# Taps between two gates, and the chunk matrices' transfers in five portions

## The chip, the cores and the metric

The kernel runs on one core of a Trainium2 chip. TensorE (PE) multiplies, VectorE (DVE), ScalarE (ACT) and GpSimd (POOL) do the rest, and SyncE (SP) issues nearly all transfers; each engine works off its own queue of instructions in program order and waits in it for what others must finish first. The metric is the time of one execution on the device in microseconds (us). The profile is taken from one execution; the median is over three others.

## The reference

One layer of a diffusion backbone over 512 latent tokens and 256 context tokens of 1024 channels: token mixing, then a mixture of 16 experts. Token mixing has two branches on the same normalised input h. One is a bidirectional diagonal state-space layer (S5: 32 groups of 16 channels, 64 complex states each), the other differential attention with 4 heads. Each branch is projected to 1024 channels and weighed by a sigmoid gate, then comes one output projection.

```python
u, q, k, v, ga, gb = split_in(h @ p['w_in'])
uc, qc, kc, vc, gac, gbc = split_in(hc @ p['w_in'])
ya, yac = s5_mixer(uc, u, p, need_ctx_out)
...
yb = diff_attention(q, concat([kc, k]), concat([vc, v]), lam, p['da_subln'], lam_init)
m = jax.nn.sigmoid(ga) * (ya @ p['w_proj_a']) + jax.nn.sigmoid(gb) * (yb @ p['w_proj_b'])
x = x + g_m * rms_norm(m @ p['w_out'], p['norm_post_mix'])
...
x = x + g_f * rms_norm(ec_moe(h2, ...), p['norm_post_ffn'])
```

The state-space layer is, in each direction, `h[l] = a * h[l-1] + B u[l]` and `y[l] = C h[l]`, both directions summed, plus a diagonal term in u.

## The kernel before

The kernel takes the 768 tokens in 96 chunks of 8. What a chunk's own inputs give to its own outputs is a product with a fixed matrix of 128 x 128 for each group (8 tokens x 16 channels on either side): the chunk matrix. It is put together from the taps, the responses C a^t B for t = 0 to 7 in either direction. What earlier and later chunks give goes through the states, which a scan over the chunks carries along.

The stages around the change, in program order: the input projection u and the factors of the taps; the chunks' states (products "st"); gates 0 to 7 (the first half of the sigmoid gates, "gate"), with the scan on VectorE and the taps between them; v for the attention ("v"); the readout ("y"), which needs the scan's end and the chunk matrices; and then the gated unit, the projections, q and k, attention, the output projection and the experts, whose weights (403 MB) stream through a ring of places.

*Numbers in two parts.* A product in float32 is made in three passes of a faster format (PASSES): each operand is split into a high part (ScalarE's copy) and a low part (VectorE's subtraction, source minus high part). For the gates, `prep_gate` (L703 to 713) does the first at once and puts the second on the list `due`, and `second_parts()` (L252) works the list off where it is called, in VectorE's queue. For v, `parts(raw, None)` (L261 to 270) does the same into a place taken from the list of free ones.

*The gates.* `gate(n)` (L722 to 740) makes 24 products of 128 x 512 in two halves and stops after each; the second half ends with the tanh (L732) and the preparation of gate n + 2. The raw weights come two gates at a time into one tile, `graw` (`load_gate`, L697): the load for gates 4 and 5 is put on `due` by gate 1, that for gates 6 and 7 by gate 3, each behind the subtraction that reads the tile last. Between the halves the loop at L888 to 917 lets VectorE go on with the scan (`steps`), from gate 2 on, and takes one piece of the taps.

*The taps.* `taps()` (L842 to 869) is a generator of eight pieces: four of the first direction (48 small products each), four of the second (16 each). After each four, ScalarE copies the result to KS (L865); in the first direction GpSimd adds the diagonal term (L868). Pieces are taken after the halves of gates 2 to 5.

*The chunk matrices.* `mt_load()` (L874 to 884) brings the taps to where the chunk matrices need them by transfers within the chip's memory, all on SP's queue: 8 from KS into the place of BZ (an operand of the taps that is no longer needed; L879), then for s = 0 to 7 two or four from BZ into the two tiles MT (L882, L884), 30 in all. They are issued after gate 5, behind two loads of v's raw weights (L915, `fetch`, L240). After that KS and BZ are given back.

*The places.* `E` is a list of free places of 128 x 2048 numbers. `take` takes the first (or, with `late=True`, the last), `give` puts places back at its end; who takes a place waits until everything that uses it from before is done. Before gate 7 `parts` takes two places for v's first two weight tiles: by the order of the list these are those of KS and BZ. v's raw tile has the place that `graw` gave back. The copies on ScalarE for both tiles stand in its queue ahead of gate 7's tanh. Two of the v accumulators are the two banks that the gates use in turn, and the first v product goes into the bank of gate 7.

Of the kernel before, what the change touches and what calls it, by code (L numbers as in the profile page):

```python
# [33 lines left out]
def layer(ctx: ExitStack, tc: tile.TileContext, A, out):  # L34
# [12 lines left out]
    ctx.enter_context(tc.manual_schedule())  # L47


    E = deque("U5 L0 L1 U7 U10 U3 U9 L2 U8 U0 U6 L3 U1 U11 L4 L5 L6 L7 U4 U2".split())  # L50
    for k in range(12):
        up.tile([128, 2048], F32, name="place", tag=f"U{k}")
    tag_of, held = {}, {}
# [1 line left out]
    def take(name, late=False):  # L55

        tag = E.pop() if late else E.popleft()
        t = (up if tag[0] == "U" else regs).tile([128, 2048], F32, name=name, tag=tag)
        tag_of[id(t)], held[id(t)] = tag, t
        return t  # L60

    def give(*ts):
        for t in ts:
            E.append(tag_of.pop(id(t)))
            held.pop(id(t))
# [23 lines left out]
    def bank(name="b"):  # L89
        turn_[0] += 1  # L90
        if three[0] and turn_[0] % 3 == 0:
            return cbank(name)
        if three[0] is None:
            return pb.tile([128, 512], F32, name=name, tag="b")
        pair_[0] += 1
        return pb.tile([128, 512], F32, name=name, tag="bd"[pair_[0] % 2])
# [143 lines left out]
    def fetch(dst, c0, p):  # L240

        DMA.dma_start(out=dst.rearrange("p (k f) -> p k f", k=2),
                      in_=w_in[256 * p:256 * p + 256, c0:c0 + 512].rearrange("(k p) f -> p k f", p=128))
# [9 lines left out]
    def second_parts():  # L253

        while due:
            due.popleft()()
# [4 lines left out]
    def parts(raw, eng, k=2):  # L261

        t = take("wp")
        hi_, lo_ = t[:, 0:1024].bitcast(F32R), t[:, 1024:2048].bitcast(F32R)
        S.activation(hi_, raw, AF.Copy)
        if eng is None:
            due.append(lambda: lo(V, lo_, raw, hi_))
        else:
            lo(eng, lo_, raw, hi_)
        return t, [v.rearrange("p (k f) -> p k f", k=k) for v in (hi_, lo_)]  # L270
# [28 lines left out]
    BC_ = take("BC")  # L299
# [162 lines left out]
    cn_ = take("cn")  # L462
# [144 lines left out]
    fm = matrices(tl)  # L607
# [86 lines left out]
    def gate_done():  # L694
        give(*GW["w"])
# [26 lines left out]
    def gate(n, eng, get):  # L722

        sg = sga_ if n < 8 else sgb_
        if n % 4 == 0:
            sg.append(take("sg"))
        w = GW["wv"][n % 2]
        pg = get("gate")
        passes(pg, w, hh, range(4), 7)
        yield  # L730
        passes(pg, w, hh, range(4, 8), 7)
        S.activation(sg[-1][:, 512 * (n % 4):512 * (n % 4) + 512], pg, AF.Tanh, scale=0.5)  # L732
        if n % 8 < 6:
            prep_gate(n + 2, eng)
        if n < 8:
            if n in (1, 3):
                due.append(lambda: load_gate(n + 3))
        elif n < 13:
            load_gate(n + 3, 1)
        yield  # L740
# [9 lines left out]
    for dr in range(2):  # L750
        for gq in range(8):
            psx = bank("st")
            pv = psx[:, 0:384].rearrange("p (g r c) -> p g r c", g=2, r=2)
            for gi in range(2):
                gp = 2 * gq + gi
                for ri in range(2):
                    for par in range(2):
                        g = 16 * (gp // 8) + 8 * par + gp % 8
# [11 lines left out]
    BZ_ = take("BZ")  # L770
# [52 lines left out]
    def steps(n):  # L823
        while n > 0:
            n -= next(fscan, 99)
# [9 lines left out]
    KS_ = take("KS")  # L835
# [6 lines left out]
    def taps():  # L842

        for dr in range(2):
            pkv = bank("K").rearrange("p (g t h) -> p g t h", g=4, t=8)
            for gi in range(4):
                def lh(q, d, ri):
                    return BZ[:, ri, 16 * d + 4 * q + gi].rearrange("p a h -> p (a h)")
                if dr == 0:

                    for d in range(2):
                        for ri in range(2):
                            for q in range(4):
                                PE.matmul(pkv[32 * q:32 * q + 32, gi, 0], lh(q, d, ri),
                                          BC[:, 1, 0, 16 * d + 4 * q + gi] if ri == 0 else CN[:, 16 * d + 4 * q + gi],
                                          start=gi == d == ri == 0, stop=d == 1 and ri == 1, skip_group_check=True)
                j1 = 1 - dr
                for ri in range(2):
                    for q in range(4):
                        PE.matmul(pkv[32 * q:32 * q + 32, gi, j1:j1 + 7].rearrange("p t h -> p (t h)"), lh(q, dr, ri),  # L860
                                  CP[dr, ri][:, 128 * (4 * q + gi) + 16 * dr:128 * (4 * q + gi) + 16 * dr + 112],
                                  start=dr == 1 and gi == ri == 0, stop=ri == 1, skip_group_check=True)
                if gi == 3:
                    t0 = slice(0, 8 - dr)
                    S.activation(KS[:, dr, :, t0], pkv[:, :, t0], AF.Copy)  # L865
                    if dr == 0:

                        GP.tensor_tensor(KS[:, 0, :, 0], KS[:, 0, :, 0], eye, op=OP.add)  # L868
                yield


    MT_ = []

    def mt_load():  # L874

        K2 = [BZ_[32 * dr:32 * dr + 32].rearrange("p (g t h) -> p g t h", g=16, t=8) for dr in range(2)]
        for dr in range(2):
            for q in range(4):
                DMA.dma_start(out=K2[dr][:, 4 * q:4 * q + 4, 0:8 - dr], in_=KS[32 * q:32 * q + 32, dr, :, 0:8 - dr])  # L879
        for s in range(8):  # L880
            for par in range(2):
                DMA.dma_start(out=MT[par][16 * s:16 * s + 16, :, s:8], in_=K2[0][16 * par:16 * par + 16, :, 0:8 - s])  # L882
                if s:
                    DMA.dma_start(out=MT[par][16 * s:16 * s + 16, :, 0:s], in_=K2[1][16 * par:16 * par + 16, :, 7 - s:7])  # L884

    ft = taps()
    wv = []
    for n in range(8):  # L888
        if n == 7:
            wv += [parts(vraw[p], None) for p in range(2)]  # L890
        for half, _ in enumerate(gate(n, None, cobank)):
            if n > 1:
                steps(1.8)
            if half == 0 and n > 1:
                second_parts()
            if n > 1:
                next(ft, None)
        if n < 2:
            second_parts()
            steps(2)  # L900
        if n == 7:
            for p in range(2):
                fetch(vraw[p], 1536, p + 2)
        if n == 5:
            for _ in ft:
                pass
            give(BC_, cn_)
            second_parts()
            give(graw)
            MT_ += [take("MT") for _ in range(2)]  # L910
            MT = [m.rearrange("p (g t h) -> p g t h", g=16, t=8) for m in MT_]
            vraw_ = take("vraw")
            vraw = [vraw_[:, 1024 * p:1024 * p + 1024] for p in range(2)]
            for p in range(2):
                fetch(vraw[p], 1536, p)  # L915
            mt_load()
            give(KS_, BZ_)
    gate_done()


# [251 lines left out]
    for p in range(4):  # L1172
        t, w = kw.pop(0)
# [303 lines left out]
    for n in range(8, 16):  # L1477
        m = n % 8
# [39 lines left out]
    hx_ = take("hfT")  # L1518
    E.extend((("SR", 0), ("U2", 0)))
    lg, aff = (keep.tile([128, 4, NE], F32, name=n) for n in ("lg", "aff"))  # L1520
# [144 lines left out]
    give(*wo, *mp_[0], *mp_[1])  # L1665
    E = deque(t for t in E if isinstance(t, tuple) or t[0] != "U")
    upper.close()
    pr = ctx.enter_context(tc.tile_pool(name="pairs", bufs=1))
    E.extend(("P", i) for i in (0, 1, 4, 2, 3, 5))
    E.extend((("SR", 1), ("gm", 0)))  # L1670

# [36 lines left out]
    def room():  # L1708

        ones_ = []  # L1710
        for tag in E:
            if is_pair(tag):
                E.remove(tag)
                t = wl[:, 0:4096] if tag[0] == "SR" else pr.tile([128, 4096], F32, name="we", tag="P%d" % tag[1])
                return t, [t[:, 0:2048], t[:, 2048:4096]], [tag]
            ones_.append(tag)
            if len(ones_) == 2:
                break
        for tag in ones_:
            E.remove(tag)  # L1720
        return None, [regs.tile([128, 2048], F32, name="wh", tag=x) if isinstance(x, str) else wl[:, 4096:6144] if x[0] == "SR" else
                      gm_ if x[0] == "gm" else yp_.rearrange("p b d -> p (b d)") for x in ones_], ones_
# [112 lines left out]
    for e in range(NE - 1):  # L1835
# [3 lines left out]
        if e % 2:  # L1839
            if not facc:  # L1840
                for x in strs(2):
                    t = regs.tile([128, 2048], F32, name="facc", tag=x)
# [26 lines left out]
    for j in range(3):  # L1869
        n = H[j].stop - H[j].start  # L1870
# [3 lines left out]
        for q in range(16 // nk):  # L1874
            if not halves:
                done_w(tags)
                _, halves, tags = room()
            wv = halves.pop(0).rearrange("p (k f) -> p k f", k=nk)
            m = 1 + (q == 1 and j == 2)
# [3 lines left out]
            for k in range(nk):  # L1883
                kt = nk * q + k
                g = kt % 2
# [71 lines left out]
```

## Time and profile before

| | |
|---|---|
| Median of 3 runs | 1576.85 us (1575.78 to 1576.99) |
| The profiled execution | 1569.68 us, its span 1567.9 us |
| TensorE busy | 1363.2 us (87%), mean granted clock 0.948 |
| VectorE, ScalarE, GpSimd busy | 523.9, 288.5, 115.1 us |
| Moved by DMA | 467.49 MB, mean 298 GB/s |
| The chain that ended last | PE 60%, DMA 22%, DVE 11%, ACT 3% of the span |

A timeline row has the start and duration in us, the engine, the line of the kernel, the operation, what it writes <- what it reads, the number of instructions merged, and in brackets the idle time before it and what ended it. PEld is TensorE's weight load, SPq SP's queue; a row of SPq is the issue of a transfer, not the transfer. PEclk is the granted clock of TensorE as a share of the full one, 2.4 GHz; the lower level is 0.5. The DMA share is the mean of 16 engines, over 1 where packets overlap.

### The profile page before, as it was taken

To read this page: it belongs to the slowest core of one execution; us is meant where nothing else is said; L and a number is where in the kernel's file an instruction comes from. 1 tells how busy PE (TensorE), PEld (TensorE's weight loads), DVE (VectorE), ACT (ScalarE), POOL (GpSimd) and SP (SyncE) were. 2 spreads that over 40 slices of the span, in tenths; PEclk is the share of its full clock that TensorE was granted. 3 is DMA by queue.
4 is the path that set the end of the run, shared out by engine and by line. 5 is a ranking of instruction groups with operands and counts; after the bars stand their busy time and mean duration, and the time that the engine had idled before them with its cause. 6 is when DMAs were issued, how large, how long until landed. Compare 5 with 4: busy or idle time off the path is not lost.

```text
span 1567.9 us, 17525 instructions
## 1 busy us (share of the span) xinstructions
PE 1363.2 (87%) x7230; PEld 733.3 (47%) x7230; DVE 523.9 (33%) x1214; ACT 288.5 (18%) x562; POOL 115.1 (7%) x87
## 2 busy tenths in 40 slices
PE   5989398998986894999999999989989979879985
PEld 3776277886665583434334343333334334324322
DVE  5789262376555647002012111111111111111103
ACT  3482004255433331100000000000000000000002
POOL 2000002332123300000000000000000000000003
PEclk9999699999997896999999999999999999999998
DMA  9111813233543248799999999999999999999994
GB/s 330 49 55 55 111 38 98 68 121 94 204 172 122 56 175 340 313 427 427 418 427 428 426 427 427 426 428 427 427 427 427 427 427 427 427 426 427 428 411 161
DMA packets 79680, 467.49 MB, mean 298 GB/s; under 512 B 14468, under 2 KB 38208, under 8 KB 49360
## 3 DMA queue, kind: packets, MB, share of 16 engines
q1 hardware_dynamic: 78288, 464.12, 74.2%
q10 hardware_dynamic: 768, 2.13, 0.4%
q8 instruction: 57, 0.93, 0.2%
q0 software_dynamic: 544, 0.12, 0.0%
q14 instruction: 23, 0.19, 0.0%
HBM read 461.66 MB, written 2.10 MB: 296 GB/s over the span
## 4 chain that ended last, share of the span: by engine, by line
PE 60%; DMA 22%; DVE 11%; ACT 3%; issue 2%; SPq 1%; POOL 0%; DVEq 0%; ACTq 0%
PE gu L1782 16%; DMA we<-in_w_exp_up_dram 11%; PE yd L1814 10%; DMA we<-in_w_exp_down_dram 7%; PE gat L1752 5%; PE gate L718 4%; PE sca L1826 4%; PE wo L1624 3%; PE u L584 2%; DMA wl<-in_w_exp_up_dram 2%; PE v L584 1%; PE k L1145 1%; PE proj L718 1%; PE o L1334 1%; PE ada L1237 1%
## 5 line engine op out<-in xcount | busy, mean ns | idle before, releaser
L1782 PE MATMUL gu<-we,gm 128*64 128x512 f32 x752 | 166.7, 595 | 16.5 <-DMA we<-in_w_exp_up_dram 10.1
L1782 PE MATMUL gu<-we,gf 128*64 128x512 f32 x752 | 167.9, 599 | 13.7 <-DMA we<-in_w_exp_up_dram 9.0
L1793 DVE TENSOR_TENSOR hid<-hid,gu 128x512 f32<-128x512 f32 x32 | 22.0, 687 | 462.9 <-PE gu L1782 462.9
L1814 PE MATMUL yd<-we,hid 128*64 128x512 f32 x688 | 152.3, 594 | 5.3 <-DMA we<-in_w_exp_down_dram 5.0
L1782 PEld LDWEIGHTS gu<-we,gm 128*64 128x64 f32 x752 | 52.9, 137 | 128.7 <-issue 104.9
L1782 PEld LDWEIGHTS gu<-we,gf 128*64 128x64 f32 x752 | 53.2, 138 | 125.6 <-issue 103.3
L718 PE MATMUL gate<-hh,wsp 128*128 128x512 f32 x384 | 98.9, 412 | 9.8 <-ACT sg L732 6.0
L1814 PEld LDWEIGHTS yd<-we,hid 128*64 128x64 f32 x688 | 49.0, 137 | 101.3 <-issue 97.1
L718 PEld LDWEIGHTS gate<-hh,wsp 128*128 128x128 f32 x384 | 73.8, 197 | 27.6 <-ACT sg L732 6.8
L1752 PE MATMUL gat<-mo,x 128*128 128x128 f32 x512 | 76.1, 313 | 10.2 <-DVE mo L1744 10.2
L1819 DVE COPY mo<-yd 64x512 f32<-64x512 f32 x15 | 10.4, 694 | 222.8 <-ACT mo L1818 222.8
L1867 POOL TENSOR_TENSOR fin<-facc,gf 128x256 f32<-128x256 f32 (+1 forms) x12 | 10.6, 913 | 997.8 <-DMA we<-in_w_exp_down_dram 993.6
L1752 PEld LDWEIGHTS gat<-mo,x 128*128 128x128 f32 x512 | 71.8, 221 | 18.1 <-issue 15.2
L1790 ACT ACTIVATE hid<-gu 128x512 f32<-128x512 f32 x32 | 19.1, 597 | 300.3 <-PE gu L1782 300.3
L1826 PE MATMUL sca<-mo,gm 128*128 128x512 f32 (+1 forms) x136 | 61.6, 591 | 4.8 <-ACT mo L1818 4.8
L1782 PE MATMUL gu<-wl,gm 128*64 128x512 f32 x208 | 53.3, 660 | 2.9 <-DMA wl<-in_w_exp_up_dram 2.9
L1798 ACT COPY hid<-ht 128x512 f32<-128x512 f32 x16 | 9.4, 585 | 249.4 <-PE ht L1797 249.4
L1624 PE MATMUL wo<-wo,mp 128*128 128x512 f32 x192 | 47.4, 404 | 2.3 <-DVE at L1484 2.3
L1818 ACT ACTIVATE mo<-yd 64x512 f32<-64x512 f32 x15 | 8.8, 589 | 214.3 <-PE yd L1814 214.3
L1831 DVE TENSOR_TENSOR facc<-facc,sca 128x512 f32<-128x512 f32 (+1 forms) x60 | 38.6, 650 | 17.7 <-PE sca L1826 17.7
L1814 PE MATMUL yd<-wl,hid 128*64 128x512 f32 x192 | 44.4, 596 | 0.0
L1826 PEld LDWEIGHTS sca<-mo,gm 128*128 128x128 f32 x136 | 21.5, 188 | 44.4 <-DVE facc L1831 23.6
(443 smaller groups left out, 1806.6 us busy)
## 6 DMA issues: line engine op xcount, KB each, us to landing
we<-in_w_exp_gate_dram SPq DMA_DIRECT2D x47, 2048.0 KB, 32.2
we<-in_w_exp_up_dram SPq DMA_DIRECT2D x47, 2048.0 KB, 28.9
we<-in_w_exp_down_dram SPq DMA_DIRECT2D x43, 2048.0 KB, 25.8
araw<-in_w_ada_dram SPq DMA_DIRECT2D x16, 1024.0 KB, 6.5
wl<-in_w_exp_gate_dram SPq DMA_DIRECT2D x8, 2048.0 KB, 28.9
wl<-in_w_exp_down_dram SPq DMA_DIRECT2D x8, 2048.0 KB, 31.0
wl<-in_w_exp_up_dram SPq DMA_DIRECT2D x8, 2048.0 KB, 26.4
wh<-in_w_exp_gate_dram SPq DMA_DIRECT2D x10, 1024.0 KB, 33.1
```

The lines of the kernel that those rows point to most:

```text
L584: PE.matmul(ps, tok(a, i, kt), w[b][:, kt % 2], start=kt == first and n == 0, stop=kt == last and n == 2)
L718: PE.matmul(ps, w[:, a, kt], x[b][kt], start=kt == 0 and n == 0, stop=kt == last and n == 2)
L1145: PE.matmul(acc[h], w[a][:, k, 128 * (h % 2):128 * (h % 2) + 128], hx[b][kt], start=kt == 0 and n == 0, stop=kt == 7 and n == 2, skip_grou ...
L1237: PE.matmul(ps[32 * j:32 * j + 32], csz[:, kt], araw[kt % 2][:, 512 * j:512 * j + 512], start=kt == 0, stop=kt == 7, skip_group_check=True)
L1624: PE.matmul(po[j], mparts(a, kt)[:, 128 * i:128 * i + 128], wo[kt][:, D * b + 512 * j:D * b + 512 * j + 512].bitcast(F32R), start=kt == 0 ...
L1752: PE.matmul(pg, x1[i][:, nb(d)], oh[:, i].rearrange("p e s -> p (e s)"), start=i == 0, stop=i == 3)
L1782: PE.matmul(pq[b][64 * j:64 * j + 64], xst[e // 2 % 2][:, kt, e % 2], wv[:, c:c + 512], start=kt == 0, stop=kt == 7, skip_group_check=True)
L1790: S.activation(hid[0][:, 1 - e % 2, b], pq[b], AF.Silu)
L1793: V.tensor_tensor(act, act, pgu[1][b], op=OP.mult)
L1814: PE.matmul(py[64 * j:64 * j + 64], hT_[:, b, i, 64 * jf:64 * jf + 64], wv[:, c:c + 512], start=(q == 0 and i == 0), stop=(q == 3 and i == ...
L1826: PE.matmul(po, gm[:, g0:g0 + 128], yp_[:, ep % 2, c], start=True, stop=True)
L1831: V.tensor_tensor(dst, dst, po, op=OP.add)
```

## The change

All eight pieces of the taps are made after gate 1, before gate 2. The tiles MT are taken there too, and `mt_load` becomes a generator that stops before s = 0, 2, 4 and 6: the 8 transfers into BZ are issued after gate 2, those for s = 0 and 1 after gate 3, s = 2 and 3 after gate 4, s = 4 and 5 after gate 5, and s = 6 and 7 after gate 6. v's first two raw loads are issued after gate 5, behind the fourth portion. KS and BZ are given back after gate 6, still ahead of the two places that v's weight tiles take before gate 7, which are again those of KS and BZ. `vraw` is taken from the list's end, the place that `graw` gave back just before. The list of places begins in another order, so that some tiles of the front part lie elsewhere, and with them the second tile of tanh values, MT, x1 and gf.

```diff
--- before.py
+++ after.py
@@ -47,7 +47,7 @@
     ctx.enter_context(tc.manual_schedule())
 
 
-    E = deque("U5 L0 L1 U7 U10 U3 U9 L2 U8 U0 U6 L3 U1 U11 L4 L5 L6 L7 U4 U2".split())
+    E = deque("U5 U11 L0 U7 U10 U3 U9 L1 U8 U0 U6 L2 U1 L3 L4 L5 L6 L7 U4 U2".split())
     for k in range(12):
         up.tile([128, 2048], F32, name="place", tag=f"U{k}")
     tag_of, held = {}, {}
@@ -878,12 +878,13 @@
             for q in range(4):
                 DMA.dma_start(out=K2[dr][:, 4 * q:4 * q + 4, 0:8 - dr], in_=KS[32 * q:32 * q + 32, dr, :, 0:8 - dr])
         for s in range(8):
+            if s % 2 == 0:
+                yield
             for par in range(2):
                 DMA.dma_start(out=MT[par][16 * s:16 * s + 16, :, s:8], in_=K2[0][16 * par:16 * par + 16, :, 0:8 - s])
                 if s:
                     DMA.dma_start(out=MT[par][16 * s:16 * s + 16, :, 0:s], in_=K2[1][16 * par:16 * par + 16, :, 7 - s:7])
 
-    ft = taps()
     wv = []
     for n in range(8):
         if n == 7:
@@ -893,28 +894,30 @@
                 steps(1.8)
             if half == 0 and n > 1:
                 second_parts()
-            if n > 1:
-                next(ft, None)
         if n < 2:
             second_parts()
             steps(2)
+        if n == 1:
+            for _ in taps():
+                pass
+            give(BC_, cn_)
+            MT_ += [take("MT") for _ in range(2)]
+            MT = [m.rearrange("p (g t h) -> p g t h", g=16, t=8) for m in MT_]
+            fm = mt_load()
+        if n > 1:
+            next(fm, None)
+        if n == 6:
+            give(KS_, BZ_)
         if n == 7:
             for p in range(2):
                 fetch(vraw[p], 1536, p + 2)
         if n == 5:
-            for _ in ft:
-                pass
-            give(BC_, cn_)
             second_parts()
             give(graw)
-            MT_ += [take("MT") for _ in range(2)]
-            MT = [m.rearrange("p (g t h) -> p g t h", g=16, t=8) for m in MT_]
-            vraw_ = take("vraw")
+            vraw_ = take("vraw", late=True)
             vraw = [vraw_[:, 1024 * p:1024 * p + 1024] for p in range(2)]
             for p in range(2):
                 fetch(vraw[p], 1536, p)
-            mt_load()
-            give(KS_, BZ_)
     gate_done()
```

## Rows read from the trace of the kernel before

**Rows 1.** Waits, all engines, 100 to 262 us: waiter, line <- releaser: sum, times, longest.

```profile
PE v L584 <- ACT sg L732: 26.5, 1, 26.5
ACT wp L265 <- DMA MT<-BZ: 23.8, 1, 23.8
```

**Rows 2.** Timeline, PE and ACT, 155 to 198 us: start, duration, engine, line, operation.

```profile
155.85 11.22 PE L718 MATMUL gate<-hh,wsp 128*128 128x512 f32 x48
156.88 0.53 ACT L865 ACTIVATE KS<-K 128x448 f32<-128x448 f32 x1
...
167.12 1.06 ACT L265 ACTIVATE wp<-vraw 128x1024 fp32r<-128x1024 f32 x1 [4.85 <-DMA BZ<-KS]
...
191.96 1.06 ACT L265 ACTIVATE wp<-vraw 128x1024 fp32r<-128x1024 f32 x1 [23.79 <-DMA MT<-BZ]
...
193.56 4.73 PE L584 MATMUL v<-wp,hc 128*128 128x512 f32 x12 [26.49 <-ACT sg L732]
```

**Rows 3.** Timeline of SP's queue, 146 to 188 us.

```profile
146.33 0.37 SPq L699 DMA_DIRECT2D graw<-in_w_in_dram  x1
158.27 0.88 SPq L242 DMA_DIRECT2D vraw<-in_w_in_dram  x2
159.26 5.99 SPq L879 DMA_DIRECT2D BZ<-KS  x8
165.82 1.87 SPq L882 DMA_DIRECT2D MT<-BZ  x3
...
170.36 0.70 SPq L882 DMA_DIRECT2D MT<-BZ  x1
...
181.31 0.62 SPq L882 DMA_DIRECT2D MT<-BZ  x1
...
186.44 1.38 SPq L884 DMA_DIRECT2D MT<-BZ  x1
```

**Rows 4.** Chain that ended last, 184 to 230 us: start, duration, what.

```profile
186.44 5.45 DMA MT<-BZ
```

**Rows 5.** DMA issues, 100 to 262 us: KB each, median us from issue to landing.

```profile
graw<-in_w_in_dram SPq DMA_DIRECT2D x3, 1024.0 KB, 5.3
vraw<-in_w_in_dram SPq DMA_DIRECT2D x4, 512.0 KB, 4.5
...
BZ<-KS SPq DMA_DIRECT2D x4, 64.0 KB, 5.1
```

**Rows 6.** Timeline, PE and DVE, 124 to 157 us, between and during the gates.

```profile
124.66 1.21 DVE L259 TENSOR_TENSOR wsp<-graw,wsp 128x1024 fp32r<-128x1024 f32 x1
...
125.93 3.98 PE L718 MATMUL gate<-hh,wsp 128*128 128x512 f32 x10 [3.32 <-DVE wsp L259]
...
128.30 1.21 DVE L259 TENSOR_TENSOR wsp<-graw,wsp 128x1024 fp32r<-128x1024 f32 x1
...
129.84 0.16 PEld L854 LDWEIGHTS K<-BC,BZ 128*32 128x32 f32 x8 [0.36 <-issue]
...
130.64 3.02 PE L718 MATMUL gate<-hh,wsp 128*128 128x512 f32 x12
...
152.80 1.22 DVE L259 TENSOR_TENSOR wsp<-graw,wsp 128x1024 fp32r<-128x1024 f32 x1 [1.96 <-ACT wsp L709]
...
155.16 1.19 DVE L786 TENSOR_TENSOR SR<-SR,mm 128x992 f32<-128x992 f32 x1
```

**Rows 7.** Stretches: busy us of PE, PEld, DVE, ACT, POOL; PEclk, DMA share, GB/s.

```profile
193.50:198.00 4.50, 4.44 (x12) 3.55 (x13) 4.19 (x21) 0.01 (x1) 0.00 (x0) 0.58 0.35 117
...
181.00:184.00 3.00, 0.00 (x0) 0.00 (x0) 0.00 (x0) 0.00 (x0) 0.00 (x0) 0.50 1.50 74
```

**Rows 8.** SP's waits, 330 to 700 us, and a stretch of the expert stage.

```profile
SPq L1732 <- PE wo L1624: 43.9, 1, 43.9
...
800.00:1000.00 200.00, 191.64 (x892) 76.12 (x890) 30.65 (x64) 12.54 (x23) 0.00 (x0) 0.99 1.01 427
```

## The prediction

> **What bounds the kernel now.** I read the waits of the stretch from the gates to the attention first, longest first. Two of them stand at one place: TensorE before its first v product and ScalarE before a copy of v's weights [rows 1]. The timeline shows how they hang together [rows 2]. Gates 6 and 7 (48 products) start at 155.85 and take 11.22 us, so TensorE is done at 167.07. On ScalarE's queue the tanh of gate 7 (L732) stands behind the two copies of v's first weight tiles (L265). The first copy runs at 167.12, the second at 191.96; the tanh comes after it, and only then is the accumulator free that v's first product takes, at 193.56. TensorE stands for 26.49 us. The second copy writes the place that BZ held, so it waits for the last transfer that reads BZ: issued at 186.44, landed 5.45 us later [rows 3, 4]. The 30 transfers of the chunk matrices, and the 8 before them, are issued from 159.26 on, because the last part of the taps is copied at 156.88 [rows 2, 3]. So what bounds this stretch is SP's queue: 38 small issues in a row, behind data that come late.
>
> **The change, part by part.** The sum is made on the profiled execution (1569.68 us, span 1567.9); the median of the runs, 1576.85, lies 7.17 above it, and I carry that difference over as it is.
>
> *The taps in one piece.* They are the same 256 products as before, now between gates 1 and 2. There TensorE stands for 3.32 us today, until the subtraction of gate 2's weights ends (124.66+1.21=125.87) [rows 6]; the last factor that the taps need is made by VectorE before that subtraction, so it is in time. A tap of the first direction takes 0.63 us (129.84 to 130.64, less 0.17 of standing) [rows 6], one of the second has a third of its products. Eight at 0.63 and a change-over on each side (0.35+0.17) are 5.5 us from 122.6, so gate 2 starts at 128 at the latest, some 2 us later than today; in return the eight interruptions of gates 2 to 5 go, each at least 0.52. That the burst of 256 keeps the pace of 48 is not shown; at twice the time gate 2 starts at 133.6. I take 5.5, since the instructions are the same. Neither is on the path: VectorE has no standstill that a tap would end, and its subtractions for gates 4 to 7 stay where they are. The one for gate 5 ends at 146.3, when the load for gates 6 and 7 is issued; the one for gate 6 ends at 152.80+1.22=154.02 [rows 3, 6]. From there two gates of 5.61 us end at 165.2 at the latest. ScalarE copies the taps before gate 2's tanh, where it waits for TensorE anyway.
>
> *The transfers in five portions.* SP serves them in program order. Portion 0 (8 issues, taps to BZ) stands behind the load for gates 4 and 5, which waits for gate 3's subtraction (128.30+1.21=129.51); by the 6.56 us from 159.26 to 165.82 it is out at 136.5. Portion 1 (s = 0, 1; 6 issues, 165.82 to 170.36) is out at 141. The load for gates 6 and 7 follows at 146.33, as today: gate 5's subtraction holds it, not the portion, with 5 us to spare [rows 3, 6]. From here on each step is on the path. From 146.70: portions 2 and 3 (16 issues, 170.36 to 181.31 today, 10.95 us) end at 157.65. v's two loads wait until gate 7's subtraction has read the gates' raw tile; on VectorE it follows the scan's step that ends at 155.16+1.19=156.35, so 157.6, nearly the same moment. The two loads take 0.99 us (158.27 to 159.26): 158.64. Portion 4 (8 issues, 5.13 us from the first, 181.31, to the last, 186.44) makes its last issue at 163.77; with 5.45 us of landing BZ is free at 169.22 [rows 3, 4, 6]. From landing to copy it is 0.07 us, from copy to v's first product 193.56-191.96=1.60: v starts at 170.9 instead of 193.56. **That is -22.7 us.** TensorE still stands 6 us before v, and v still starts at the lower level of 1.2 GHz (0.58 granted over its first 4.5 us today) [rows 7]: no gain and no loss from the clock.
>
> Bounds of this chain. From below: 0.61 us per issue and nothing between them, and a landing of 4.5, that of v's loads [rows 5]; v at 169.1, and 1.9 us more if its first 12 products (4.73 us [rows 2]) run at the later 0.234: -26.4. From above: each group of issues waits in the DMA engines for the load in front of it (5.3 for the gates', 4.5 for v's [rows 5]): 146.33+5.3+10.95+4.5+5.13+5.45=177.7, v at 179.3: -14.2. I take the measured pitch and landing: the 8 issues that follow v's two loads directly today landed in 5.1 [rows 5], so loads ahead in the queue have cost little.
>
> The last landing is the term that the Trainium skill prices otherwise. "DMA: Bandwidth & Descriptors", section "Anatomy of one DMA", has about 2.0 us plus bytes/436e9 for a transfer (measured for another way of issuing, so an estimate here): 2.3 us for these 112 KB, and -25.9 in all. The row says 5.45, and I go by the row; the page's result is rival 3. Its section "Queues, rings and completion order" says that each DMA engine takes descriptors in ring order, which speaks against small transfers behind big loads: rival 1.
>
> *The rest.* v's raw tile had the gates' place before too, so taking it from the other end of the list changes nothing by itself. The new order of the free places gives the second tanh tile the place of cn, and the matrices those of WT and BC, all read for the last time by the taps or before. After v everything is one chain: the scan on VectorE (its next piece stands behind the same weights), readout, attention, expert weights. SP's first full expert load waits 43.9 us for products of the output projection, and the stream then runs at 427 GB/s: bound by transfers, but started by TensorE [rows 8]. So the whole gain reaches the end: 1569.68-22.7=1547.0 in the profile, **1576.85-22.7=1554.2** as median.
>
> **The rivals.**
> *1. The portions queue behind the big loads in the DMA engines* (chance 0.13). For it: late in the transfers the engines' share is 1.50, more than one packet in each [rows 7]. Against it: the 5.1 us behind v's loads [rows 5]. Time: v between 173.9 (landing not counted again) and 179.3: 1557.2 to 1562.6, middle 1560.
> *2. TensorE becomes the bound* (0.08). It stands some us before gates 4 and 6; if the clock falls there and stays at 1.2 GHz over both last gates, 48 products of 0.398 end at 173.1, v follows at 173.7: -19.9, 1557.0. Against it: after the 3.32 us only ten products were slow (3.98 us), 1.6 us in all [rows 6], and gate 7 would still be hidden.
> *3. Shorter landings* (0.06): -25.9, 1551.0.
> *4. No gain* (0.03): the copy waits on its place for another reason than these transfers, or a later transfer takes the gain back: 1576.9. For the second a transfer between 200 and 600 us would have to start by itself; SP's longest wait there names TensorE [rows 8].
> *5. Slower* (0.04). x1, gf and three of the free places that the expert weights turn through lie elsewhere. If that slowed the stream of 403 MB (16 experts of three 1024x2048 matrices of 4 bytes) from 427 GB/s, the gain would be gone at 417 (943 us become 966); at 412 the time is 1588. Against it: 427 is held whichever place is filled [rows 8].
>
> **How the numbers follow.** The forecast has 0.66, from 1552 to 1557. The range that should hold 8 in 10 takes in rivals 2 and 3 and the nearer half of rival 1: 1549.5 to 1561. Faster by over 0.2% (3 us, about what this measurement can tell from no change) are the forecast and rivals 1 to 3: 0.93; within 0.2%: 0.03; slower: 0.04.
>
> **What would show it.** The taps as one block before gate 2, without 3.3 us of standing; SP's issues of the chunk matrices in groups from about 137 to 164; ScalarE's second copy of v's weights at about 169 and v's first product at about 171; then every stage 22 to 23 us earlier. It is wrong if that copy waits to 174 or later, if the load for gates 6 and 7 is issued clearly after 146.4, if gate 7 ends after 169, or if the shift at v is not there at the end.

## The result, and the profile after

| kernel | median us of the runs | beside it, before | ratio (95% interval) | profiled execution, its span |
|---|---|---|---|---|
| changed, first comparison | 1554.9 (1553.47 to 1559.93) | 1576.92 (1575.78 to 1577.93) | 0.9866 [0.9843, 0.9890] | 1559.93, 1558.2 |
| changed, second comparison | 1555.38 (1552.82 to 1557.58) | 1574.67 (1571.53 to 1579.01) | 0.9876 [0.9858, 0.9893] | span 1553.6 |
| changed, third comparison | 1555.48 (1551.58 to 1557.36) | 1575.70 (1565.89 to 1579.06) | 0.9881 [0.9855, 0.9908] | span 1553.1 |

The change makes the kernel 1.2 to 1.3% faster, 19.3 to 22.0 us. 1554.2 was forecast. The place of the gain is the one forecast; its size at that place is not, as the profile shows.

The waits of the changed kernel, 100 to 262 us, in the columns of [rows 1]; lines behind the loop of the gates are numbered 3 higher than before:

```profile
PE v L584 <- ACT sg L732: 10.4, 1, 10.4
ACT wp L265 <- DMA MT<-BZ: 6.9, 1, 6.9
```

Both waits of [rows 1] are still there, 16.1 and 16.9 us shorter. The same pair, the same order: ScalarE's second copy for v still waits for BZ's place, and TensorE waits for the tanh behind that copy. TensorE's timeline (start, duration, line, operation, in brackets the idle time before and what ended it) answers to [rows 2] and [rows 6]:

```profile
122.93 0.26 PE L854 MATMUL K<-BC,BZ 128*32 128x16 f32 x8
...
125.20 2.10 PE L860 MATMUL K<-CP,BZ 128*32 128x112 f32 x78
127.23 11.63 PE L718 MATMUL gate<-hh,wsp 128*128 128x512 f32 x50
141.82 13.96 PE L718 MATMUL gate<-hh,wsp 128*128 128x512 f32 x48 [2.96 <-DVE wsp L259]
156.20 10.72 PE L718 MATMUL gate<-hh,wsp 128*128 128x512 f32 x46 [0.42 <-DVE wsp L259]
177.29 5.16 PE L584 MATMUL v<-wp,hc 128*128 128x512 f32 x12 [10.37 <-ACT sg L732]
```

The taps begin at 122.93 and gate 2 at 127.23, without standing: 4.3 us for the burst (granted clock 1.00 from 123 to 128), and the standstill of 3.32 before gate 2 [rows 6] is gone. Gate 7 ends at 166.92. v starts at 177.29 instead of 193.56. ScalarE between them:

```profile
167.75 1.06 ACT L265 ACTIVATE wp<-vraw 128x1024 fp32r<-128x1024 f32 x1 [5.63 <-DMA vraw<-in_w_in_dram]
175.70 1.06 ACT L265 ACTIVATE wp<-vraw 128x1024 fp32r<-128x1024 f32 x1 [6.89 <-DMA MT<-BZ]
176.66 0.58 ACT L732 ACTIVATE sg<-gate 128x512 f32<-128x512 f32 x1
```

SP's queue in the changed kernel, beside [rows 3]: the load for gates 6 and 7 (L699), the chunk matrices (L884, L886), v's two loads (L242).

```profile
147.17 0.39 SPq L699 DMA_DIRECT2D graw<-in_w_in_dram  x1
147.60 0.59 SPq L884 DMA_DIRECT2D MT<-BZ  x1
...
151.91 0.61 SPq L884 DMA_DIRECT2D MT<-BZ  x1
153.76 0.58 SPq L886 DMA_DIRECT2D MT<-BZ  x1
...
160.64 1.54 SPq L242 DMA_DIRECT2D vraw<-in_w_in_dram  x2
162.50 0.59 SPq L884 DMA_DIRECT2D MT<-BZ  x1
163.38 2.16 SPq L886 DMA_DIRECT2D MT<-BZ  x1
...
168.75 0.61 SPq L884 DMA_DIRECT2D MT<-BZ  x1
171.33 0.58 SPq L886 DMA_DIRECT2D MT<-BZ  x1
```

The last issue was forecast for 163.77; it comes at 171.33, after two gaps (151.91 to 153.76, 168.75 to 171.33) that [rows 3] did not have. What filled them stands in SP's own waits, 146 to 176 us (sum, times, longest):

```profile
SPq L699 <- DVE wsp L259: 4.5, 1, 4.5
SPq L886 <- DMA vraw<-in_w_in_dram: 2.0, 1, 2.0
SPq L886 <- DMA graw<-in_w_in_dram: 1.2, 1, 1.2
SPq L884 <- DMA MT<-BZ: 1.2, 3, 0.6
SPq L242 <- DVE sp L813: 1.0, 1, 1.0
```

and in the chain that ended last (start, duration, what):

```profile
147.17 6.58 DMA graw<-in_w_in_dram
153.75 0.02 issue
...
161.70 9.61 DMA vraw<-in_w_in_dram
171.32 0.02 issue
171.33 4.29 DMA MT<-BZ
```

A transfer of the chunk matrices reads nothing of graw or vraw, and still its issue waits for their landing: 147.17+6.58=153.75 and 161.70+9.61=171.31. Counted in SP's timeline, the issue that waits is each time the eighth behind the load; the last section says what holds it.

The first products of the stages, from the traces of these kernels (us):

| kernel | v | readout, from the states (L968) | gated unit | k (first weights) | output projection | last expert's output, first product | span |
|---|---|---|---|---|---|---|---|
| before, first profile | 193.6 | 221.3 | 254.8 | 291.7 | 541.6 | 1528.1 | 1567.9 |
| before, again | 191.7 | 220.2 | 253.7 | 290.6 | 538.4 | 1524.8 | 1566.2 |
| taps alone | 192.8 | 220.9 | 254.4 | 292.9 | 545.0 | 1531.5 | 1573.0 |
| changed, first | 177.3 | 205.5 | 239.1 | 277.6 | 529.8 | 1516.5 | 1558.2 |
| changed, second | 174.3 | 202.7 | 236.2 | 274.6 | 526.9 | 1513.7 | 1553.6 |
| changed, third | 175.3 | 203.6 | 237.1 | 275.5 | 524.9 | 1511.5 | 1553.1 |
| changed, second copy late | 169.9 | 198.4 | 232.0 | 268.8 | 515.4 | 1502.0 | 1543.7 |

### The profile page after: what moved, and what is told of

It is laid out like the page before. It is cut to its first block, busy times and chain, and to the rows that moved or that the text cites. A ratio compares the mean times of both kernels' runs of the same rounds, so it can differ in the third digit from the quotient of the medians.

```text
span 1558.2 us, 17528 instructions
## 1 busy us (share of the span) xinstructions
PE 1367.1 (88%) x7230; PEld 739.3 (47%) x7230; DVE 525.7 (34%) x1214; ACT 288.8 (19%) x562; POOL 114.9 (7%) x87
## 4 chain that ended last, share of the span: by engine, by line
PE 57%; DMA 24%; DVE 13%; ACT 3%; issue 2%; SPq 1%; POOL 0%; DVEq 0%; ACTq 0%
PE gu L1785 15%; DMA we<-in_w_exp_up_dram 11%; PE yd L1817 10%; DMA we<-in_w_exp_down_dram 8%; PE gat L1755 5%; PE sca L1829 4%; PE wo L1627 3%; PE gate L718 3%; DMA wl<-in_w_exp_up_dram 2%; PE u L584 2%; PE v L584 2%; PE k L1148 1%; PE proj L718 1%; PE o L1337 1%; PE ada L1240 1%
## 5 line engine op out<-in xcount | busy, mean ns | idle before, releaser
L1822 DVE COPY mo<-yd 64x512 f32<-64x512 f32 x15 | 10.4, 694 | 221.2 <-ACT mo L1821 221.2
```

## The experiments

My theory after the first profile: the mechanism is the one forecast, the chain on SP's queue was priced too short, and what is left of the wait is still BZ's place. Against it stood two questions: whether the changed schedule loses time behind v (there the first two profiles differ by 6.5 us: v to the span's end 1374.3 before, 1380.9 after), and whether the taps, the spacing of the portions or the loads for v carry the effect.

**The two kernels again.** Both unchanged, with a new profile each and many timed runs.

> The kernel before once more, for a second profile. In the first comparison the median fell by 22.0 us, but the two profiled executions differ by only 9.8 (1569.68 and 1559.93), though v's first product moved by 16.3. Theory A: a single execution varies by some us outside the changed stretch, mostly where TensorE's granted clock falls; then this profile has the state products' start at 98 to 99 and v's first product at 193 to 195 as before, but stages behind it that are 3 to 7 us longer than in the first profile, or differ at other places. Theory B: the changed kernel loses 6 us in the stages behind v by itself; then this profile repeats the first one's stages behind v within 1 us.

> The changed kernel once more. Theory A: from the state products to v's first product 78 us again (within 1.5), v's gap of about 10 us behind the tanh of gate 7, and in the stages behind v other lengths than in the first profile of the change (+0.6 to the gated unit, +1.6 to k, +2.4 from the scores to the output projection, +1.7 at the end). Theory B: the same losses at the same places. Median 1553 to 1557 by both.

Measured: before 1573.14 against 1574.67 for itself (ratio 0.9988 [0.9975, 1.0001]); changed 1555.38 (0.9876). From v to the span's end it is again 1374.6 and 1379.3. That alone looked like a loss in the changed kernel. The next kernel says otherwise.

**The taps alone.** The taps stand between gates 1 and 2 as in the change; all portions are issued behind v's loads, as before.

```diff
-        if n > 1:
-            next(fm, None)
-        if n == 6:
-            give(KS_, BZ_)
...
             for p in range(2):
                 fetch(vraw[p], 1536, p)
+            for _ in fm:
+                pass
+            give(KS_, BZ_)
```

> The changed kernel with the taps in one piece before gate 2, but all 38 transfers issued after gate 5 behind v's loads, as before the change. Theory: the taps are off the path and the gain is the transfers' alone; SP's issues run from about 159 to 187, v's first product at 192 to 194, the time 1574 to 1578, no difference from before. Rival: the eight interruptions of the gates cost TensorE time that counts; then 4 to 6 us less than before, 1571 to 1573.

Measured: 1574.95, ratio 1.0000 [0.9988, 1.0012]. TensorE's row at v:

```profile
192.79 5.00 PE L584 MATMUL v<-wp,hc 128*128 128x512 f32 x12 [28.00 <-ACT sg L732]
```

The taps are worth nothing by themselves: the gates end earlier and TensorE stands 28.00 us instead of 26.49. And this kernel, with before's time, takes 1380.2 us from v to the end, as long as the changed one. So a loss of 6.5 us in the changed schedule is ruled out, to within the interval of some 2 us: before's two profiles caught short executions (1569.68 and 1568.03, where its medians are 1573 to 1577).

**All transfers at once behind gate 2.**

```diff
-        if n > 1:
-            next(fm, None)
+        if n == 2:
+            for _ in fm:
+                pass
```

> The changed kernel with all 38 transfers issued in one go after gate 2. Theory: SP's queue is in order, so the load for gates 6 and 7 comes behind them, at about 158 instead of 146 to 147; the subtraction of gate 6 ends at about 166, gate 7 at 176 to 179, and v starts at 177 to 181, 2 to 5 us later than in the changed kernel: 1556 to 1561. Rival: the spacing has no effect, since BZ is free early; then v starts at 168 to 170 and the time is 1547 to 1549.

Measured: 1565.58, ratio 0.9947 [0.9926, 0.9967]; worse than I expected. SP first, then ScalarE's copy of the gates' weights, then TensorE, each from its own timeline:

```profile
159.82 0.53 SPq L699 DMA_DIRECT2D graw<-in_w_in_dram  x1
```

```profile
167.34 1.06 ACT L709 ACTIVATE wsp<-graw 128x1024 fp32r<-128x1024 f32 x1 [19.55 <-DMA graw<-in_w_in_dram]
```

```profile
168.45 14.11 PE L718 MATMUL gate<-hh,wsp 128*128 128x512 f32 x48 [15.91 <-ACT wsp L709]
183.25 3.01 PE L584 MATMUL v<-wp,hc 128*128 128x512 f32 x12 [0.69 <-ACT sg L732]
```

Here the load for gates 6 and 7 stands behind all the small transfers and is issued at 159.82 instead of 147.17; TensorE waits 15.91 us before gate 6, and v starts at 183.25. The wait has moved from v to gate 6. The five portions are what keeps that load in its time: more than half of the gain hangs on the spacing.

**v's loads behind portion 4.** This takes v's loads out from in front of the last portion.

```diff
         if n == 6:
             give(KS_, BZ_)
+            for p in range(2):
+                fetch(vraw[p], 1536, p)
...
-            for p in range(2):
-                fetch(vraw[p], 1536, p)
```

> The changed kernel with both of v's first loads behind the last portion of the chunk matrices' transfers instead of in front of it. In both profiles of the change the last issue came at 169.2 and 171.3, not at the predicted 163.8, and it waited for a load of v that had been issued eight issues earlier. Theory: each issue waits until the transfer eight issues before it has landed, so a big load in front holds a small transfer eight places behind; then the last issue of the portions comes at 164 to 166 here, BZ is free at 169 to 171, but v's loads now land at 171 to 174 and v's first product is at 174 to 177, so the time stays within 1553 to 1558. Rival: the small transfers fill the DMA engines by themselves; then the last issue stays at 168 to 171 and v goes to 177 or later.

Measured: 1556.33, ratio 0.9893 [0.9871, 0.9916]. SP and ScalarE:

```profile
162.35 2.38 SPq L884 DMA_DIRECT2D MT<-BZ  x1
...
167.79 0.83 SPq L886 DMA_DIRECT2D MT<-BZ  x1
168.73 8.76 SPq L242 DMA_DIRECT2D vraw<-in_w_in_dram  x4
```

```profile
173.50 1.06 ACT L265 ACTIVATE wp<-vraw 128x1024 fp32r<-128x1024 f32 x1 [10.27 <-DMA vraw<-in_w_in_dram]
```

No issue of a portion waits for v's loads now. The last one comes at 167.79, 3.5 us earlier than in the changed kernel's first profile and 1.4 earlier than in its second, and still 4 us behind the forecast. So v's loads are one part of the excess and not all of it: one issue still waits 2.3 us for the gates' load, and an issue of over 2 us (162.35) is there without them too. The copy now waits for v's load itself, and nothing is gained in time. How the excess divides between the waits for a landing and the fill of the DMA engines (share 1.20, 1.39, 1.01 in 3 us each from 158 on in the changed kernel) is settled only so far.

**The second copy behind the tanh of gate 7.** If the rest of the wait is BZ's place, the tanh need only stand ahead of the copy that waits for it: then TensorE starts v on its first part and the second part comes in time.

```diff
         if n == 7:
-            wv += [parts(vraw[p], None) for p in range(2)]
+            wv += [parts(vraw[0], None)]
+            wt = take("wp")
...
         if n == 7:
-            for p in range(2):
-                fetch(vraw[p], 1536, p + 2)
+            fetch(vraw[0], 1536, 2)
+            w1 = [wt[:, 1024 * r:1024 * r + 1024].bitcast(F32R) for r in range(2)]
+            S.activation(w1[0], vraw[1], AF.Copy)
+            steps(5)
+            lo(V, w1[1], vraw[1], w1[0])
+            wv.append((wt, [x.rearrange("p (k f) -> p k f", k=2) for x in w1]))
+            fetch(vraw[1], 1536, 3)
...
-        steps(5)
+        if p:
+            steps(5)
```

> The changed kernel with the tanh of gate 7 ahead of the second copy of v's weights, and that copy's subtraction behind the scan steps of v's first part. Theory: what is left of the wait before v is the place of BZ alone, read by the last transfer, with TensorE done at 167. Then v's first product starts after the first copy, at 168 to 170 instead of 177.3, VectorE's wait of 6.7 us before the second subtraction goes, and the time is 6 to 8 us below the changed kernel, 1547 to 1549. Rival: the transfers of the chunk matrices themselves, or the scan on VectorE, set the readout's start; then v starts earlier but the readout does not, and the time stays at 1554 to 1556.

Measured: 1547.87, ratio 0.9828 [0.9807, 0.9850]; 7.5 us less than the changed kernel on the same chip. ScalarE and TensorE:

```profile
168.29 1.06 ACT L265 ACTIVATE wp<-vraw 128x1024 fp32r<-128x1024 f32 x1 [4.66 <-DMA vraw<-in_w_in_dram]
169.25 0.58 ACT L732 ACTIVATE sg<-gate 128x512 f32<-128x512 f32 x1
174.81 1.06 ACT L915 ACTIVATE wp<-vraw 128x1024 fp32r<-128x1024 f32 x1 [4.98 <-DMA MT<-BZ]
```

```profile
169.89 0.49 PE L584 MATMUL v<-wp,hc 128*128 128x512 f32 x1 [1.45 <-ACT sg L732]
...
180.69 2.83 PE L584 MATMUL v<-wp,hc 128*128 128x512 f32 x11 [1.48 <-DVE wp L259]
```

The copy still waits for BZ until 174.81, but TensorE works on v's first part meanwhile, and 1.48 us are left in front of the second. v starts at 169.9, close to where it was forecast, by another order.

**The same order on the kernel before,** to see whether it does this by itself; the edit is the one above.

> The kernel before with one edit only: the tanh of gate 7 ahead of the second copy of v's weights, and that copy's subtraction behind the scan steps of v's first part. Theory: the transfers still land at 190 to 192, so v's first part (36 products, 9 to 10 us) moves into the standstill, v's first product comes at 168 to 171, and v's second part waits for the copy until 193 to 195: 8 to 10 us less than before, 1564 to 1567. Rival: the order on ScalarE's queue was the whole loss; then the time is that of the changed kernel or less, 1547 to 1556.

Measured: 1564.30, ratio 0.9950 [0.9930, 0.9969]. TensorE:

```profile
168.46 0.50 PE L584 MATMUL v<-wp,hc 128*128 128x512 f32 x1 [1.36 <-ACT sg L732]
...
192.94 0.79 PE L584 MATMUL v<-wp,hc 128*128 128x512 f32 x1 [13.88 <-ACT wp L905]
```

v starts even earlier, and its second part waits for BZ 13.88 us. The order alone is worth 8.0 us and the earlier transfers alone 19.3 to 22.0; both together 26.8, and 28.2 on the third chip below.

**v's second load behind portion 4, with the late copy.** The last step that looked open: only the half of v's load that is needed first stays in front of the last portion.

```diff
         if n == 6:
             give(KS_, BZ_)
+            fetch(vraw[1], 1536, 1)
...
-            for p in range(2):
-                fetch(vraw[p], 1536, p)
+            fetch(vraw[0], 1536, 0)
```

> The changed kernel with the tanh of gate 7 ahead of the second copy, as in the run before, and v's second load behind the last portion, only the first in front of it. Theory: v's first copy waited for its load until 168.3 there, which shared the DMA engines with the second load and the portions; alone it lands at 164 to 166, so v starts right behind gate 7, at 167 to 168.5, 1.5 to 3 us earlier, 1544.5 to 1547. Rival: VectorE's scan sets the readout's start by now; then v starts earlier and the time stays within 1547 to 1549.

Measured: 1553.47, ratio 0.9879 [0.9857, 0.9902], with single runs from 1545.65 to 1554.33. ScalarE:

```profile
168.51 1.06 ACT L265 ACTIVATE wp<-vraw 128x1024 fp32r<-128x1024 f32 x1 [7.74 <-DMA MT<-BZ]
```

The first copy starts at 168.51 instead of 168.29: nothing gained. The row names a transfer of the chunk matrices as what ended its wait, but v's first load, issued at 159.21, landed 9.28 us later, at 168.49, just ahead of the copy, and the transfer that the row means, issued at 165.09, landed only at 170.32. So the copy waited for v's load as before, and that load, now without the second behind it, took longer than the 6.85 us of the run before, not less as I had expected. As the runs lay 9 us apart, three kernels were timed side by side on a third chip.

> The changed kernel, for a comparison on one chip with the two that follow: 1553 to 1557, v's first product at 174 to 178, and 16 to 20 us less than before in the time.

> The changed kernel with the tanh of gate 7 ahead of the second copy, once more: v at 168.5 to 170.5, 5 to 9 us below the changed kernel by the theory that the wait on BZ's place is what is left; if its first result (7.5 us) was the chance of TensorE's clock in the stages behind v, within 2 us of the changed kernel.

> The same with v's second load behind the last portion. On another chip it was 18.9 us below the kernel before in the unprofiled runs, against 26.8 for the version with both loads in front; its profile showed no earlier v (170.1), since the copy then waited for the small transfers' landing. Theory: it is no better than the version before it, within 3 us of it or above; rival: its 1545.7 in one execution is what it can do, and it comes out 2 us or more below.

Measured: changed 1555.48, late copy 1547.53 (ratio 0.9832 [0.9805, 0.9858]), late copy and split 1550.48 (0.9865 [0.9834, 0.9895]). The late copy without the split is the fastest of the kernels timed: 8.0 us below the changed kernel here, 7.5 on the other chip, and 1.7% below before on both.

## Why the prediction came out

*What bounds the kernel.* Right. TensorE stands before v because ScalarE's tanh stands behind a copy that waits for BZ's last reader; with the tanh moved ahead of that copy, TensorE starts v 4 to 8 us earlier.

*The taps.* Right. 4.3 us against a bound of 5.5, at full pace, off the path: the kernel with the taps alone has before's time.

*The load for gates 6 and 7.* Right. Issued at 147.17 (145.81 in the second profile, 146.07 in the third; in the first the state products already start 0.8 us later than in before), held by VectorE's subtraction (4.5 us of SP's waiting) and not by portion 1. Gate 7 ended at 166.92, 1.7 later than the 165.2 forecast and before the limit of 169.

*The chain of portions 2 to 4.* This is the step that was mis-sized: 17.07 us forecast from the first issue to the last, 23.7, 22.9 and 24.0 measured. The sign that I had named for it, the second copy at 174 or later, came in the first profile (175.70); in the second and third the copy came at 172.75 and 173.68, still 3.5 and 4.4 us behind the forecast of 169.3. Forecast and measured, in the three profiles:

| step | forecast | first | second | third |
|---|---|---|---|---|
| first issue of portion 2 | 146.70 | 147.60 | 146.24 | 146.49 |
| to v's loads | 10.95 | 13.04 | 13.78 | 12.89 |
| v's loads | 0.99 | 1.86 | 1.26 | 1.63 |
| portion 4, first to last issue | 5.13 | 8.83 | 7.88 | 9.47 |
| landing of the last | 5.45 | 4.29 | 3.52 | 3.12 |
| landing to v's first product | 1.67 | 1.67 | 1.66 | 1.67 |
| v | 170.9 | 177.29 | 174.34 | 175.27 |

The issues were priced at before's pitch [rows 3]. In the changed kernel the eighth issue behind a load waits for its landing, and the loads took 6.6 and 9.6 us to land where [rows 5] has 5.3 and 4.5. Of the 6.7 us in the first profile, 3.2 went to the two waits for loads, 1.5 to waits for the portions' own earlier landings, 1.0 to v's second load, which waited for VectorE, and 1.5 to one issue of 2.16 us; the other issues ran some 0.5 us quicker than forecast. What misled me was the row that I used against rival 1: the issues behind v's loads in before landed in 5.1 us [rows 5] (the median of four of them; for the other four it is 3.4). There the price was not to be seen: v's second load landed 5.46 us after its issue, at 164.15, and the eighth issue behind it came at 164.64, so it had nothing to wait for.

In the changed kernel loads and small transfers both land later where portions of the chunk matrices are in flight beside a load. The gates' load took 6.6 us with portion 2 right behind it and 5.3 in before with nothing behind it; the eight transfers of portion 2 landed after 6.1 to 7.6 us, and after 4.0 to 4.4 in before. With nothing but one another behind them, in the kernel with v's loads behind portion 4, v's two loads landed in 4.8 and 5.4 us. The eight transfers into BZ did less: behind v's loads in before they left these at 3.9 and 5.5. How the DMA engines divide their time between the two is not shown by these runs. v came at 177.3, 174.3 and 175.3, where rival 1 (173.9 to 179.3) had it, and its mechanism is seen in these landings; what rival 1 did not have is that a late landing reaches the chain through the issues in SP's queue that wait for it.

*The last landing.* The measured 4.29, 3.52 and 3.12 us lie between the row (5.45) and the estimate from the Trainium skill, "DMA: Bandwidth & Descriptors", section "Anatomy of one DMA" (2.3). For this transfer the estimate is too small and the one row was on the long side; the runs of these kernels decide for 3.1 to 5.5.

*Why the median was met all the same.* In part by luck. The shift at v is 17.0 us (mean of three profiles each, those of before and of the taps alone against the changed kernel's: 192.7 to 175.6), not 22.7, so 5.7 us of the forecast gain did not come where it was forecast. The timed gains, 22.0, 19.3 and 20.2 us, are 2 to 5 us more than this shift, and that remainder is in no term of the sum; it made up for most of the error in the first comparison and for less than half of it and just over half in the other two. The first profile of before does not show it: it lay 7.17 us below its median, and against it the changed kernel's span is only 9.7 to 14.8 us shorter. Against the profile of the kernel with the taps alone, which lies at its median (1574.8 to 1574.95), the span of the changed kernel is 14.8 to 19.9 us shorter, 18.0 on average, and that is its shift at v (192.8 to 175.6: 17.2) within 1 us. So the profiles have the gain at v and nowhere else; the remainder of the timed gains lies within the spread of single executions (up to 10 us from their median), and where it comes from stays open.

*The rivals that fell.* TensorE as the bound: gates 4 and 5 took 13.96 us, 2.7 more than 48 products in [rows 2], and gate 7 still ended 10.4 us before v. No gain and slower: from the first product that gathers tokens for the experts (L1752) to the first of the last expert's output it is 904.2 to 905.1 us in every profile here, so the new places of the tiles cost nothing.

## What to carry to other kernels

When a small transfer is moved among large ones, its issue has a price of its own: look in the waits of the issuing queue for a landing that the transfer does not need, and count which issue pays it (here the eighth). A wait on a chain of instructions can be cut at two ends, by making its data earlier or by letting what stands behind it go first; here the two ends add up (about 20 and 8 us, against 27 to 28 for both), and the second was an order of three instructions. Before the profile of one execution is used as the base of a sum, its time belongs beside the median: here it lay 7 us below, and what it was short by lay far behind the change.

## What the runs showed of the hardware

*The eighth issue.* Wherever SP's issue of a small transfer waited for a load that it does not read, it was the eighth issue behind that load: 153.76 for the load of 147.17 and 171.33 for v's second, issued at about 161.7, in the first profile of the changed kernel, and in its second profile 152.53 for 145.81 and 169.16 for v's second load, issued at about 160.6:

```profile
160.59 8.55 DMA vraw<-in_w_in_dram
169.14 0.02 issue
169.16 3.52 DMA MT<-BZ
```

With v's loads behind the portions the same holds among the small ones: the issue at 162.35 waits for the one of 156.12, eight before it, which landed after 6.22 us. It holds all through: in none of the 13 traces does one of SP's 371 issues start before the transfer eight issues ahead of it has landed, while 123 to 143 in each trace start before the one seven ahead has. The records of the issues say why: they raise eight completion semaphores, in turn but for a few places, and an issue that waits names the semaphore that it will raise itself. So at most eight transfers of SP's queue are in flight in these kernels. That belongs to the programs as they were built; whether the chip would carry more is not shown here. It also prices the small transfers alone: at the pitch of 0.65 us eight issues take 5.2 us, and where the landings take longer, as the 6.1 to 7.6 us of portion 2, the issues wait for them.

*The clock after the same standstill.* Between the gated unit and k, the profiles take 36.8 to 36.9 us or 38.4 to 38.5, in kernels with the same instructions there. TensorE in before and in the changed kernel's second profile, at the projection:

```profile
270.33 0.73 PE L718 MATMUL proj<-ya,wpr 128*128 128x512 f32 x2 [0.22 <-DVE ya L113]
271.59 0.49 PE L718 MATMUL proj<-ya,wpr 128*128 128x512 f32 x1 [0.53 <-ACT ya L112]
272.32 4.38 PE L718 MATMUL proj<-ya,wpr 128*128 128x512 f32 x18 [0.23 <-DVE ya L113]
```

```profile
251.65 0.73 PE L718 MATMUL proj<-ya,wpr 128*128 128x512 f32 x2 [0.23 <-DVE ya L113]
252.91 0.50 PE L718 MATMUL proj<-ya,wpr 128*128 128x512 f32 x1 [0.53 <-ACT ya L112]
253.64 4.61 PE L718 MATMUL proj<-ya,wpr 128*128 128x512 f32 x12 [0.23 <-DVE ya L113]
```

The standstills are the same to 0.01 us; then one takes 0.243 us for a product and the other 0.384. The granted clock (the column ahead of the last two) in the two stretches:

```profile
272.70:274.70 2.00, 2.00 (x10) 1.65 (x9) 0.69 (x1) 0.64 (x1) 1.09 (x1) 1.00 0.00 0
```

```profile
254.10:256.10 2.00, 2.00 (x7) 1.58 (x6) 0.69 (x1) 0.63 (x1) 1.17 (x1) 0.53 0.00 0
256.10:258.10 2.00, 2.00 (x7) 1.55 (x7) 0.00 (x0) 0.00 (x0) 0.11 (x1) 0.61 0.00 0
```

One is granted 2.4 GHz after these standstills, the other near 1.2 GHz for about 4 us: 1.6 us in all. The kernel with the taps alone has the slow form, and so have all three profiles of the changed kernel; both of before and both of the late copy have the fast one. So at this place no kernel was seen in both forms, and the runs do not show whether the form goes with the kernel or with the execution.

One stage earlier the same kernel was seen in both. The two profiles of the late copy take 34.9 and 36.5 us from the readout's first product, the one on the chunk matrices (197.1 and 195.1), to the gated unit's; the granted clock is 1.00 throughout that stage in the first, and 0.78 and 0.80 in the 8 us from 199 on in the second. The Trainium skill, "TensorE: Matmul & The Clock Gate", section "Part 1: The HAM clock gate (the "warmup" mystery)", says that the number of slow products varies from run to run for the same kernel; these two profiles agree. Of the 13 profiles nine lose some 1.5 us at one of these two places, none at both and four at neither. What decides it is not settled here; for comparing kernels it means that a difference of some 2 us in one pair of profiles is not yet an effect of a change.
